# A hybrid decoder layer on one core: left-side tiles moved up by 128 bytes, and attention's small tiles in a pool of their own

## The chip, the cores and the metric

The kernel runs on one core of one Trainium2 chip. Its time is the device time of one execution, in microseconds (us); lower is better. TensorE (PE) multiplies, and its weight loads are listed apart as PEld; VectorE is DVE, ScalarE is ACT, GpSimd is POOL, and SyncE (SP) issues the DMAs.

## The reference

One layer over 1024 tokens of width 1024, all in float32. `A` are eight heads with a sliding window of 128, ALiBi and sinks, `B` are eight heads of causal attention with a forget gate; both read one projection of RMSNorm(x).

```python
xn = rmsnorm(x, attn_norm_g)
proj = jnp.einsum('bsd,de->bse', xn, w_in)
qa, ka, va, qb, kb, vb, f_logit = jnp.split(proj, IN_SPLITS, axis=-1)
...
out_a = swa_sinks_attention(qa, ka, va, sink_logits)
...
out_b = forgetting_attention(qb, kb, vb, log_f)
mixed = jnp.concatenate([out_a.reshape(b, s, A_Q_W), out_b.reshape(b, s, B_W)], axis=-1)
x = x + jnp.einsum('bse,ed->bsd', mixed, w_out)
hn = rmsnorm(x, mlp_norm_g)
hid = jnp.square(jax.nn.relu(jnp.einsum('bsd,df->bsf', hn, w_up)))
x = x + jnp.einsum('bsf,fd->bsd', hid, w_down)
```

## The kernel before

**Arithmetic.** Each float32 product is three passes in float32r: both operands are split into a high and a low part (`split`, lines 73 to 78), and hi·hi, hi·lo and lo·hi are added up in PSUM. All products go through the helper `mm` (line 71), so they stand under L71 and are told apart by their tiles. In `mm(out, lhsT, rhs)` the second argument is the stationary operand, loaded as weights before each matmul, and the third is the moving operand, streamed past it; most moving tiles are 512 columns wide.

**Stages.** The first projection (`qps`, lines 162 to 192) and the later ones (`ps`, function `proj`) take tokens `xh`, `xl` as weights and the split weights `wh`, `wl` as moving tiles of 384 or 392 columns. Attention's scores (`sp`, `spb`) take queries (`q1a`, `q1b`) as weights, and keys (`k1a`, `k1b`, and their low part `k2z`) move. The probabilities are turned by transposes (`tpa`, `tpb`), in which the probabilities are the weights and `ident` moves. The turned ones (`pth`, `ptl`) move past the values `va`, `vb` (`pv`, `pvb`). The output projection (`po`) takes `wos` as weights past `mix`. Both halves of the MLP are done by Strassen-Winograd products, seven for eight. Up (`up`, line 969 onwards) runs 16 steps `j`; each makes seven pairs of weights `wu`, four blocks of 128 columns, and moves `bh` and `bl` past them: 84 matmuls of 512 columns into `pu`, in the order wu hi·bh, wu hi·bl, wu lo·bh. Down (`down`) runs 16 steps over four phases; per product it splits `hx` and `wx` and makes 24 matmuls of 512 columns into `pd`, in the same order of three. Both have 1344 matmuls.

**Where tiles lie.** In a partition of SBUF, pools with `side="left"` stack upwards and pools with `side="right"` stack down from byte 229,344; a tile's bytes are rounded up to 32. The left side begins at byte 2,176 with pool `cp`, whose tiles come in the order of their declarations: `ident`, `ident_b`, `ones1`, `vt` (36 floats, 160 bytes with rounding), then nothing larger than 256 bytes, 2,528 bytes in all. So the pools behind it (`xg_p` and `wp`, later `zl` in their place) begin at byte 4,704, which is 96 modulo 256. All slots of `zl` are multiples of 2,048 bytes long: everything in it, `wu`, `wos`, `mix` and the left-side slots of `hx` and `wx` among it, begins at 96 modulo 256. On the right side `ap1` (q, k, v after projection; `va`, `vb`) holds multiples of 256 bytes and lies at 224 modulo 256. `ap2` under it mixes large tiles with small ones of 4 to 64 bytes: in between these, `q1a`, `q1b` and the bias tiles come to lie at 64 modulo 256, and `k1a`, `k1b`, `k2z`, `pth`, `ptl` and the probabilities at 192. Pool `zr`, which takes the place of `ap1` and `ap2` after attention, holds multiples of 256 bytes again: `bh`, `bl` and the right-side slots of `hx` and `wx` lie at 224. `ident` lies at 128.

In `down` a set of `hx` and `wx` is always from one pool: the first four sets alternate left, right, left, right (`FIRST`), and after them all are on the left (`SETS`).

**What sets the order.** The program's order is laid by a planner that plays the kernel on a timeline of its own and takes what is ready by priority; `tc.high_priority` and `tc.issue_after` push and hold, and `PACE` spreads the projections over attention. A tile waits for a free slot of its tag, and tiles of `zl` and `zr` wait for those earlier tiles that lay at the same bytes (`reuse_waits="tile"`).

Of the kernel before, what the change touches and what calls it, by code (L numbers as in the profile page):

```python
# [8 lines left out]
F32 = mybir.dt.float32  # L9
# [7 lines left out]
P = 128  # L17
# [3 lines left out]
NT = S // P  # L21
HD = 64
NH = 8
# [30 lines left out]
def hybrid_layer(  # L54
# [13 lines left out]
    nc = tc.nc  # L68

    def mm(out, lhsT, rhs, start, stop):  # L70
        return nc.tensor.matmul(out, lhsT, rhs, start=start, stop=stop)  # L71
# [20 lines left out]
    cp = ctx.enter_context(tc.tile_pool(name="cp", bufs=1))  # L92
# [8 lines left out]
    ones1 = cp.tile([P, 1], F32, name="ones1")  # L101
    nc.vector.memset(ones1, 1.0)

    vt = cp.tile([P, 36], F32, name="vt")
    nc.scalar.dma_start(vt, vecs)
    nc.scalar.preload_act_table_set("natural_log_exp_and_others")
    ga, gm, vec, bfb, snk = (
        vt[:, a:b] for a, b in ((0, 8), (8, 16), (16, 20), (20, 28), (28, 36))
# [31 lines left out]
    at = ExitStack()  # L140
    ap1 = at.enter_context(tc.tile_pool(name="ap1", bufs=1, side="right"))
    ap2 = at.enter_context(tc.tile_pool(name="ap2", bufs=1, side="right"))
    maskd = ap2.tile([P, P], F32, tag="mt", name="maskd", bufs=2)
    nc.gpsimd.memset(maskd, 0.0)
    nc.gpsimd.affine_select(
# [82 lines left out]
    def qknorm(x, nh, tlo, thi, r=None):  # L228


        n = thi - tlo
        w = nh * HD
        sq = ap2.tile([P, 1024], F32, tag="sq", name="sq", bufs=1)
        sqv = sq[:, : n * w].rearrange("p (t c) -> p t c", t=n)
        xv = x[:, tlo:thi, :w]
        nc.gpsimd.tensor_tensor(out=sqv, in0=xv, in1=xv, op=ALU.mult)
        ss, r0, u = (
            ap2.tile([P, 16], F32, tag=tag, name=tag, bufs=2)[:, : n * nh]
            for tag in ("ss", "sr0", "su")
        )  # L240
        nc.vector.tensor_reduce(
            out=ss, in_=sq[:, : n * w].rearrange("p (g d) -> p g d", d=HD),
            axis=AX.X, op=ALU.add,
        )
        th = lambda a: a.rearrange("p (t h) -> p t h", h=nh)
        nc.vector.scalar_tensor_tensor(
            out=th(ss), in0=th(ss), scalar=1.0 / HD,
            in1=ep2[:, tlo:thi].unsqueeze(2).to_broadcast([P, n, nh]),
            op0=ALU.mult, op1=ALU.add,
        )  # L250
        nc.scalar.activation(r0, ss, AF.Ln)
        nc.scalar.activation(r0, r0, AF.Exp, scale=-0.5)
        nc.vector.tensor_tensor(out=u, in0=r0, in1=r0, op=ALU.mult)
        nc.vector.tensor_tensor(out=u, in0=u, in1=ss, op=ALU.mult)
        na = nh + (2 if r is not None else 0)
        if r is None:
            rv = ap2.tile([P, 16], F32, tag="r", name="r", bufs=2)[:, : n * nh]
            rv = th(rv)
        else:
            rv = r[:, tlo:thi, :]  # L260
        nc.vector.scalar_tensor_tensor(
            out=rv[:, :, :nh], in0=th(u), scalar=3.0, in1=th(r0),
            op0=ALU.subtract, op1=ALU.mult,
        )
        for t in range(n):
            xt = x[:, tlo + t, : na * HD].rearrange("p (h d) -> p h d", d=HD)
            nc.gpsimd.tensor_tensor(
                out=xt, in0=xt, in1=rv[:, t].unsqueeze(2).to_broadcast([P, na, HD]), op=ALU.mult
            )
# [110 lines left out]
    for t in range(0, NT, 4):  # L380
        qknorm(q0, 4, t, t + 4, rqk)
# [41 lines left out]
    def forget_gates():  # L423
        zf = z.rearrange("p h t -> p (h t)")

        zt = ap2.tile([P, 4, NT * NH], F32, tag="sq", name="zt", bufs=1)
        ze, zs, zp = zt[:, 0], zt[:, 1], zt[:, 2]
        nc.vector.scalar_tensor_tensor(out=ze, in0=zf, scalar=-1.0, in1=zf, op0=ALU.mult, op1=ALU.min)
        nc.scalar.activation(ze, ze, AF.Exp)
        nc.vector.tensor_scalar(out=zs, in0=ze, scalar1=2.0, scalar2=None, op0=ALU.add)  # L430
        nc.vector.reciprocal(zs, zs)
        nc.vector.tensor_tensor(out=zs, in0=zs, in1=ze, op=ALU.mult)
        nc.vector.tensor_tensor(out=ze, in0=zs, in1=zs, op=ALU.mult)
        nc.vector.tensor_scalar_mul(zp, ze, 2.0 / 17.0)
        for n in (15, 13, 11, 9, 7, 5, 3):
            nc.vector.scalar_tensor_tensor(
                out=zp, in0=zp, scalar=2.0 / n, in1=ze, op0=ALU.add, op1=ALU.mult
            )
        nc.vector.scalar_tensor_tensor(out=zp, in0=zp, scalar=2.0, in1=zs, op0=ALU.add, op1=ALU.mult)
        nc.vector.scalar_tensor_tensor(  # L440
            out=zt[:, 3], in0=zf, scalar=0.0, in1=zp,
            op0=ALU.min, op1=ALU.subtract,
        )
        pt = pa.tile([P, 512], F32, tag="tr", name="ptf", bufs=2)
        nc.tensor.transpose(pt[: NH * NT, :P], zt[:, 3], ident)
        cum = ap2.tile([NH * NT, P], F32, tag="rdt", name="cum", bufs=1)
        nc.vector.tensor_tensor_scan(
            out=cum, data0=ones1[: NH * NT].to_broadcast([NH * NT, P]),
            data1=pt[: NH * NT, :P], initial=0.0, op0=ALU.mult, op1=ALU.add,
        )  # L450
        off = pa.tile([P, 512], F32, tag="tr", name="off", bufs=2)
        mm(
            off[: NH * NT, 0:1], before.rearrange("p h t -> p (h t)"),
            cum[:, P - 1 : P], True, True,
        )
        offs = ap2.tile([NH * NT, 1], F32, name="offs")
        nc.vector.tensor_copy(offs, off[: NH * NT, 0:1])
        nc.vector.tensor_scalar(
            out=cum, in0=cum, scalar1=offs[:, 0:1], scalar2=None, op0=ALU.add
        )  # L460
        nc.sync.dma_start(c_d.rearrange("h (t q) -> (h t) q", q=P), cum)
# [163 lines left out]
    def scores_b(p, qp, h):  # L625
        q1, k1, k2, cb = heads[p, "q"][h], heads[p, "k1", h], k2_of[h], heads[p, "cb", h]
        probs = []
        for i in (2 * qp, 2 * qp + 1):
            nk = (i + 1) * P
            pr = ap2.tile(  # L630
                [P, S if i > 3 else 512], F32, tag="s" if i > 3 else "u", name="sb",
                bufs=NS if i > 3 else NU,
            )
            nm = ap2.tile([P, 4], F32, tag="nm", name="nmb", bufs=4)
            dn = ap2.tile([P, 4], F32, tag="dn", name="dnb", bufs=4)
            qs = q1[:, i * P : (i + 1) * P]
            for c in range((nk + 511) // 512):
                n = min(512, nk - c * 512)
                ne = max(n, 256)
                ks = slice(c * 512, c * 512 + ne)  # L640
                sp = pa.tile([P, 512], F32, tag="sc", name="spb", bufs=2)
                last = (c + 1) * 512 >= nk
                mm(sp[:, :ne], qs, k1[:, ks], True, False)
                mm(sp[:, :ne], qs, k2[:, ks], False, not last)
                if last:
                    pe = mm(sp[:, n - P : n], ident_b, mask_b, False, True)
                nc.vector.tensor_tensor_reduce(  # L647
                    out=pr[:, c * 512 : c * 512 + n], in0=sp[:, :n],
                    in1=cb[:, c * 512 : c * 512 + n], scale=1.0,
                    scalar=3e38 if c == 0 else nm[:, 0:1],  # L650
                    op0=ALU.add, op1=ALU.min, accum_out=nm[:, c : c + 1],
                )
            nc.scalar.activation(
                pr[:, :nk], pr[:, :nk], AF.Exp, scale=-1.0, bias=nm[:, c : c + 1],
                accum_out=dn_b[p % 2][:, h, i : i + 1] if p < 3 else dn[:, 0:1],
            )
            probs.append(pr)
            if p < 3:
                continue
            nc.vector.reciprocal(dn[:, 1:2], dn[:, 0:1])  # L660
            if i > 1:
                nc.vector.tensor_scalar_mul(pr[:, :nk], pr[:, :nk], dn[:, 1:2])
            else:
                nc.gpsimd.tensor_tensor(
                    out=pr[:, :nk], in0=pr[:, :nk],
                    in1=dn[:, 1:2].to_broadcast([P, nk]), op=ALU.mult,
                )
        marks.append(pe.ins)
        return probs
# [221 lines left out]
    left, right = slice(0, 512), slice(512, 1024)  # L891
# [328 lines left out]
    for i in range(len(STEPS)):  # L1220
        down(i)
        if STEPS[i][0] == len(PHASES) - 1 and late:
            name, dt, cs = late.pop(0)
# [63 lines left out]
```

## Time and profile before

| | us |
|---|---|
| three runs: lowest, median, highest | 1122.52, 1126.16, 1127.7 |
| the profiled execution | 1124.34 |
| its span, first to last instruction | 1122.6 |
| up in the chain that ended last (`pu`, two pieces) | 181.77 and 117.12 |
| down in the same chain (`pd`) | 300.64 |

The profile is of one execution. Its busy time counts an engine as busy while an instruction's record lasts; matmul records overlap, since each begins before the record of the one ahead has ended. So the pace of a stretch of matmuls is read from the stretch's length and its count, and not from the mean record. The chain that ended last is followed back from the last instruction, each time to what released it. A matmul's row by tile gives the shortest, the median and the longest record.

### The profile page before, as it was taken

To read this page: it belongs to the slowest core of one execution; us is meant where nothing else is said; L and a number is where in the kernel's file an instruction comes from. 1 tells how busy PE (TensorE), PEld (TensorE's weight loads), DVE (VectorE), ACT (ScalarE), POOL (GpSimd) and SP (SyncE) were. 2 spreads that over 40 slices of the span, in tenths; PEclk is the share of its full clock that TensorE was granted. 3 is DMA by queue.
4 is the path that set the end of the run, shared out by engine and by line. 5 is a ranking of instruction groups with operands and counts; after the bars stand their busy time and mean duration, and the time that the engine had idled before them with its cause. 6 is when DMAs were issued, how large, how long until landed. Compare 5 with 4: busy or idle time off the path is not lost.

```text
span 1122.6 us, 15570 instructions
## 1 busy us (share of the span) xinstructions
PE 1098.7 (98%) x5551; PEld 937.5 (84%) x5551; DVE 765.4 (68%) x1311; ACT 575.4 (51%) x1013; POOL 361.0 (32%) x338
## 2 busy tenths in 40 slices
PE   9999998999999999899999999999999999999998
PEld 8999988799997888777888887888888888888886
DVE  7476665765667577699867677855575876674395
ACT  5567557766677656455454534344444433333331
POOL 4751613335434545124232323222221222222100
PEclk9999999999999999999999999999999999999999
DMA  9311302314438656473454544335699786665523
GB/s 312 124 36 37 95 24 59 96 29 142 153 120 312 203 182 219 168 236 131 173 194 169 196 151 159 134 121 194 227 392 351 258 299 244 216 230 205 173 95 113
DMA packets 95710, 195.68 MB, mean 174 GB/s; under 512 B 7136, under 2 KB 19088, under 8 KB 95632
## 3 DMA queue, kind: packets, MB, share of 16 engines
q1 hardware_dynamic: 95488, 194.66, 49.6%
q8 instruction: 44, 0.72, 0.3%
q14 instruction: 34, 0.28, 0.1%
q10 hardware_dynamic: 144, 0.02, 0.0%
HBM read 141.61 MB, written 53.04 MB: 173 GB/s over the span
## 4 chain that ended last, share of the span: by engine, by line
PE 83%; DVE 7%; issue 4%; DMA 4%; POOL 1%; ACT 1%; SPq 0%; DVEq 0%; ACTq 0%; POOLq 0%
PE pd L71 27%; PE pu L71 27%; PE ps L71 12%; PE po L71 4%; PE qps L71 3%; PE spb L71 3%; PE pvb L71 2%; PE tpb L683 2%; PE sp L71 1%; DVE ptl L360 1%; DMA mixs_d<-mixs 1%; DVE sb L647 1%; DVE bl L78 1%; PE pv L71 1%; DMA wr<-in_w_b_dram 1%
## 5 line engine op out<-in xcount | busy, mean ns | idle before, releaser
L71 PE MATMUL pd<-hx,wx 128*128 128x512 f32 x1344 | 304.9, 389 | 0.0
L71 PEld LDWEIGHTS pd<-hx,wx 128*128 128x128 f32 x1344 | 252.3, 188 | 52.4
L71 PE MATMUL pu<-bh,wu 128*128 128x512 f32 x896 | 281.6, 395 | 0.8 <-ACT wu L75 0.8
L71 PEld LDWEIGHTS pu<-bh,wu 128*128 128x128 f32 x896 | 168.8, 188 | 40.7 <-ACT wu L75 1.2
L71 PE MATMUL pu<-bl,wu 128*128 128x512 f32 x448 | 176.9, 395 | 0.5 <-DVE bl L78 0.5
L75 ACT CAST hx<-hr 128x1024 fp32r<-128x1024 f32 x56 | 59.0, 1054 | 176.2 <-PE pd L71 171.3
L78 POOL TENSOR_TENSOR wx<-wda,wx 128x1024 fp32r<-128x1024 f32 x24 | 64.5, 2687 | 197.0 <-ACT wx L75 197.0
L78 DVE TENSOR_TENSOR hx<-hr,hx 128x1024 fp32r<-128x1024 f32 x56 | 72.7, 1305 | 73.5 <-ACT hx L75 73.4
L71 PE MATMUL ps<-wh,xh 128*128 128x384 f32 (+1 forms) x320 | 110.2, 345 | 0.3 <-ACT qkb L600 0.3
L71 PE MATMUL ps<-wh,xl 128*128 128x384 f32 (+1 forms) x320 | 109.3, 342 | 0.0
L71 PE MATMUL ps<-wl,xh 128*128 128x384 f32 (+1 forms) x320 | 109.1, 342 | 0.0
L71 PEld LDWEIGHTS pu<-bl,wu 128*128 128x128 f32 x448 | 84.4, 188 | 21.1 <-DVE bl L78 0.9
L71 PE MATMUL po<-mix,wos 128*128 128x512 f32 x384 | 95.8, 400 | 3.7 <-DMA mix<-mixs_d 1.6
L78 POOL TENSOR_TENSOR wu<-wus,wu 128x512 fp32r<-128x512 f32 x32 | 48.0, 1501 | 133.4 <-ACT wu L75 133.4
L71 PEld LDWEIGHTS po<-mix,wos 128*128 128x128 f32 x384 | 70.9, 190 | 18.3 <-DMA mix<-mixs_d 1.8
L75 ACT CAST wu<-wus 128x512 fp32r<-128x512 f32 x64 | 39.0, 618 | 79.4 <-PE pu L71 76.0
L78 POOL TENSOR_TENSOR wu<-wur,wu 128x512 fp32r<-128x512 f32 x32 | 43.3, 1354 | 88.2 <-ACT wu L75 88.2
L360 DVE TENSOR_TENSOR ptl<-tpb,pth 128x512 fp32r<-128x512 f32 (+1 forms) x80 | 50.0, 632 | 25.9 <-ACT pth L359 25.2
L965 DVE TENSOR_TENSOR ht<-hb 128x512 f32<-128x512 f32 x32 | 21.8, 722 | 64.7 <-ACT hb L1020 64.7
L78 POOL TENSOR_TENSOR wl<-wr,wh 128x384 fp32r<-128x384 f32 (+1 forms) x47 | 49.9, 1076 | 48.8 <-ACT wh L75 36.9
L75 ACT CAST wx<-wda 128x1024 fp32r<-128x1024 f32 x56 | 58.3, 1044 | 7.2 <-DMA wda<-in_w_d_dram 6.6
L71 PEld LDWEIGHTS ps<-wh,xh 128*128 128x128 f32 x320 | 60.4, 189 | 1.1 <-ACT qkb L600 0.6
(218 smaller groups left out, 2058.4 us busy)
## 6 DMA issues: line engine op xcount, KB each, us to landing
wda<-in_w_d_dram SPq DMA_DIRECT2D x34, 1024.0 KB, 9.0
hr<-hid_d SPq DMA_DIRECT2D x56, 512.0 KB, 5.8
wur<-in_w_u_dram SPq DMA_DIRECT2D x32, 512.0 KB, 4.4
hid_d<-ht SPq DMA_DIRECT2D x16, 1024.0 KB, 4.3
hid_d<-hb SPq DMA_DIRECT2D x16, 768.0 KB, 3.6
mixs_d<-mixs SPq DMA_DIRECT2D x14, 512.0 KB, 3.4
mix<-mixs_d SPq DMA_DIRECT2D x7, 1024.0 KB, 8.7
wr<-in_w_b_dram SPq DMA_DIRECT2D x32, 192.0 KB, 2.4
```

Of the source, the lines that this page charges most:

```text
L71: return nc.tensor.matmul(out, lhsT, rhs, start=start, stop=stop)
L75: hi_eng.copy(hi, src)
L78: lo_eng.tensor_tensor(out=lo, in0=src, in1=hi.bitcast(F32), op=ALU.subtract)
L360: nc.vector.tensor_tensor(out=lo[:, cols], in0=pt[:, cols], in1=hi[:, cols].bitcast(F32), op=ALU.subtract)
L647: nc.vector.tensor_tensor_reduce(out=pr[:, c * 512 : c * 512 + n], in0=sp[:, :n], in1=cb[:, c * 512 : c * 512 + n], scale=1.0, scalar=3e38 ...
L683: nc.tensor.transpose(tp[:, c0 : c0 + P], probs[qi][:, kb * P : (kb + 1) * P], ident)
L965: eng.tensor_tensor(out=out, in0=a, in1=b, op=ALU.subtract)
```

## The change

`vt` is made 68 floats wide instead of 36, of which the load and all readers still use the first 36. With rounding it grows from 160 to 288 bytes, so that all that stands behind it on the left side lies 128 bytes further: the pools behind `cp` begin at 4,832, or 224 modulo 256. `ident`, `ident_b`, `ones1` and `vt` itself stay where they are. The small tiles of `ap2` (`ss`, `sr0`, `su`, `r`, `offs`, `nm`, `dn`; 800 bytes) go to a new pool `ap3`, opened after `ap2` and so under it. All that stays in `ap2` then lies at 224 modulo 256. `ap1` and `zr` stay where they are. No instruction is added, removed or moved in the text of the program.

```diff
-    vt = cp.tile([P, 36], F32, name="vt")
-    nc.scalar.dma_start(vt, vecs)
+
+
+    vt = cp.tile([P, 68], F32, name="vt")
+    nc.scalar.dma_start(vt[:, :36], vecs)
...
     ap2 = at.enter_context(tc.tile_pool(name="ap2", bufs=1, side="right"))
+
+    ap3 = at.enter_context(tc.tile_pool(name="ap3", bufs=1, side="right"))
...
-            ap2.tile([P, 16], F32, tag=tag, name=tag, bufs=2)[:, : n * nh]
+            ap3.tile([P, 16], F32, tag=tag, name=tag, bufs=2)[:, : n * nh]
             for tag in ("ss", "sr0", "su")
...
-            rv = ap2.tile([P, 16], F32, tag="r", name="r", bufs=2)[:, : n * nh]
+            rv = ap3.tile([P, 16], F32, tag="r", name="r", bufs=2)[:, : n * nh]
...
-        offs = ap2.tile([NH * NT, 1], F32, name="offs")
+        offs = ap3.tile([NH * NT, 1], F32, name="offs")
...
-            nm = ap2.tile([P, 4], F32, tag="nm", name="nmb", bufs=4)
-            dn = ap2.tile([P, 4], F32, tag="dn", name="dnb", bufs=4)
+            nm = ap3.tile([P, 4], F32, tag="nm", name="nmb", bufs=4)
+            dn = ap3.tile([P, 4], F32, tag="dn", name="dnb", bufs=4)
```

Distances between the moving operand and the weights, modulo 256:

| matmuls | columns | before | after |
|---|---|---|---|
| `pu` (up) | 512 | 128 | 0 |
| `pd` (down), `po` | 512 | 0 | 0 |
| `pd`, the last matmul of each of the first four sets, against the next set's weights | 512 | 128 | 0 |
| `pv`, `pvb` | 512, 256 | 32 | 0 |
| `sp`, `spb` | 256 to 512 | 128 | 0 |
| `qps`, `ps` | 384, 392 | eight values, in steps of 32 | the same eight |
| transposes of probabilities | 128 | 64 | 96 |

## The prediction

> **What bounds the kernel now.** I read the page first: who is busy, and of what the chain that ended last is made.
>
> ```profile
> PE 1098.7 (98%) x5551; PEld 937.5 (84%) x5551; DVE 765.4 (68%) x1311; ACT 575.4 (51%) x1013; POOL 361.0 (32%) x338
> ...
> PE 83%; DVE 7%; issue 4%; DMA 4%; POOL 1%; ACT 1%; SPq 0%; DVEq 0%; ACTq 0%; POOLq 0%
> PE pd L71 27%; PE pu L71 27%; PE ps L71 12%; PE po L71 4%; PE qps L71 3%; PE spb L71 3%; PE pvb L71 2%; PE tpb L683 2%; PE sp L71 1%; DVE ptl L360 1%; DMA mixs_d<-mixs 1%; DVE sb L647 1%; DVE bl L78 1%; PE pv L71 1%; DMA wr<-in_w_b_dram 1%
> ```
>
> PE carries 83% of the chain, and up and down carry 27% each. So the next view is the chain in order of time, from the start of up (start, length, what, how many).
>
> ```profile
> 512.40 181.77 PE pu L71 x781
> 694.17 1.72 PE pms L71 x4
> 695.88 117.12 PE pu L71 x504
> 813.01 300.64 PE pd L71 x1326
> 1113.67 0.71 DVE pd L1204
> ```
>
> From 512 us to 1114 us PE waits for nobody: what a matmul there costs is what the kernel costs. The two stages do the same kind of matmul, 512 columns in three float32r passes, and do not run at the same pace. Up: 181.77 + 117.12 = 298.89 us for 1285 matmuls, 232.6 ns each. Down: 300.64 us for 1326, 226.7 ns each. So the question is why a matmul of up takes 5.9 ns more, and whether the change takes that away.
>
> **Is it other engines' traffic?** Next come windows of 20 us: busy time and count by engine, granted clock, DMA share, GB/s. The first two lie in up, the others in down.
>
> ```profile
> 740.00:760.00 20.00, 20.00 (x88) 16.22 (x87) 12.24 (x18) 8.93 (x11) 5.64 (x5) 1.00 0.42 156
> 780.00:800.00 20.00, 20.00 (x88) 16.21 (x87) 10.10 (x17) 7.74 (x10) 3.88 (x3) 1.00 0.36 133
> 820.00:840.00 20.00, 20.00 (x90) 16.56 (x89) 14.63 (x12) 5.74 (x6) 5.87 (x2) 1.00 1.05 393
> 1080.00:1100.00 20.00, 20.00 (x90) 16.57 (x89) 20.00 (x18) 7.67 (x8) 0.00 (x0) 1.00 0.56 194
> ```
>
> The clock is 1.00 in all four. Down holds its 90 matmuls with the DMAs full (1.05) and POOL at work, and with DVE busy for the whole window; up gets 88 with DVE at half and DMA at 0.36. Other engines' load does not explain it. What differs is where the operands lie: in down both are at one offset modulo 256, in up they are 128 apart.
>
> **Does the offset itself show?** The records by tile (shortest, median, longest, ns) stand below for up, down, and attention's product with the values. The two-matmul row is down again, in a window of 0.2 us around the end of its first set: the next set's weights are on the other side.
>
> ```profile
> L71 PE MATMUL pu<-bh,wu x896: 390/393/797, 496.7 to 812.6; 128*128 128x512 f32 x180
> ...
> L71 PE MATMUL pd<-hx,wx x1344: 388/389/398, 812.8 to 1117.3; 128*128 128x512 f32 x192
> ...
> L71 PE MATMUL pv<-pth,va x30: 388/398/506, 86.5 to 211.2; 128*128 128x512 f32 x30
> ...
> L71 PE MATMUL pd<-hx,wx x2: 389/392/396, 817.9 to 818.1; 128*128 128x512 f32 x2
> ```
>
> Down, at distance 0, has a median of 389; up, at 128, has 393. In the two-matmul row one record of 389 stands beside one of 396: the same tiles and stage, and the only matmul there during which weights 128 apart are loaded costs 7 more. That crossing also changes sides, so I look for a case on one side: `pv` has both operands on the right, 32 apart, and its median is 398. Unequal offsets cost, then, also without a change of side, though attention's rows hold stalls too.
>
> **Part 1, the left side 128 bytes further.** The distance in up goes from 128 to 0. If its matmuls then run at down's pace, 1285 × 226.7 ns = 291.3 us take the place of 298.89: 7.6 us less, all of it on the chain. The 59 other matmuls of up's 1344 lie before 512.40, where the chain runs through DVE: I count nothing for them. The four crossings in down are worth 4 × 7 ns, nothing.
>
> What is late next, if PE runs 2.5% faster? The window over up's longer piece, and the longest wait for PE in up:
>
> ```profile
> 513.00:694.00 181.00, 181.00 (x780) 146.76 (x779) 131.41 (x195) 85.97 (x110) 54.92 (x38) 1.00 0.46 167
> ...
> ACT wu L75 <- PE pu L71: 102.0, 52, 2.2
> ```
>
> The busiest other engine in up is DVE, 131.41 of 181 us; it would rise from 73% to about 75%. The weight splits on ACT wait for PE to give slots back (102.0 us in 52 waits), so the feed has slack. The tightest spot is the start of down, which moves 7.6 us ahead:
>
> ```profile
> 808.32 1.05 ACT L75 CAST wx<-wda 128x1024 fp32r<-128x1024 f32 x1 [5.37 <-DMA wda<-in_w_d_dram]
> ...
> L78 POOL TENSOR_TENSOR wx<-wda,wx x3: 2412/2605/3368, 801.0 to 821.7; 128x1024 fp32r<-128x1024 f32 x3
> ```
>
> The second set's weights are cast at 808.32, after 5.37 us of waiting for their DMA, and POOL adds at most 3.4 us: ready at about 813, used at 818.1. That is 5 us of cover. The slots that these loads wait for come free in the last step of up, so they move ahead with it; only the part of up's gain that falls after the release is lost to the loads, 84 × 5.9 ns = 0.5 us for a whole step. The cover holds. If it were gone, PE would stand still once for what is missing, not for every set.
>
> **Part 2, attention's tiles at one offset.** 156 matmuls of 512 columns go from 32 or 128 apart to 0: 60 in `pv`, 48 each in `spb` with `k1b` and `k2z`.
>
> ```profile
> L71 PE MATMUL spb<-k2z,q1b 128*128 128x512 f32 x48 | 19.0, 396 | 0.0
> ...
> L683 PE MATMUL tpb<-ident,sb 128*128 128x128 f32 x288 | 44.6, 273 | 0.1
> L288 PE MATMUL ptq<-ident,q 128*128 128x128 f32 x32 | 5.5, 273 | 0.0
> ...
> L71 PE MATMUL sp<-k1a,q1a x64: 274/281/389, 58.1 to 176.4; 128*128 128x256 f32 x64
> ...
> L71 PE MATMUL pvb<-pth,vb x160: 277/281/415, 212.6 to 459.8; 128*128 128x256 f32 x160
> ```
>
> At 396 and 398 against 389 they cost 7 to 9 ns too much: 156 × 8 = 1.2 us, of which I take 0.5, because attention's chain changes often between PE, DVE and POOL. The 256-wide ones (`sp`, `pvb`, some of `spb`, about 500) have no row at equal offsets; from median to shortest is 281 − 274 = 7 ns, so ±3.6 us of PE time and about a third of that on the chain; I take 0 and keep ±1.2 for the range. The transposes go from 64 to 96 apart; `ptq` turns tiles of `ap1`, which are 96 apart already, at the same 273 ns: no price.
>
> **What has one answer.** `qps`, `ps`, `po` and down's own pairs keep their distances. VectorE, ScalarE and GpSimd work from tiles at new addresses; ScalarE's casts of `wh` go through eight offsets already, and all lie close together:
>
> ```profile
> L75 ACT CAST wh<-wr x40: 498/512/525, 25.7 to 273.4; 128x384 fp32r<-128x384 f32 x32, 128x392 fp32r<-128x392 f32 x8
> ...
> L896 ACT ACTIVATE bh<-h,vt x10: 707/722/725, 462.1 to 497.4; 128x512 fp32r<-128x512 f32 x10
> ...
> 429.93 0.97 POOL sb L664 x2
> ```
>
> The new pool changes one order: `ap3` lies under slot c0 of `zr`, so `bh1` now waits for the last reader of `nm` and `dn`. That is the scaling of the last probabilities, on DVE and POOL; POOL's piece stands in the chain at 429.93, and `bh` is first written at 462.1. It costs nothing.
>
> **Sum.** 7.6 + 0.5 = 8.1 us off: the profiled execution (1124.34, that is 1.7 around its span) goes to 1116.2. The median of the three runs, 1126.16, is 1.8 above the profiled one; on that footing the forecast is 1118. About 0.5%, 5.6 us, is what a measurement of this kernel can tell from no change.
>
> **The rivals.** *The offset is not the cause* (0.16). In down, operands at distance 0 modulo 256 are at 0 modulo 512 too, since their slots are multiples of 2,048 apart and their steps are 512; in up the change leaves them 256 apart modulo 512 (4,832 + 40,960 against 100,320), and on two sides. If 512 counts, or the side, up stays at 232.6 ns and the time at 1124.3, or 1126 as a median, less at most attention's 1.2. For it: only the crossing and attention separate the offset from the stage, and neither separates it cleanly. Against it: `pv` on one side. The Trainium skill speaks for this rival: its page "TensorE: Matmul & The Clock Gate", section "Step-by-step: what each phase is for", gives PE two independent read ports and says that loading the next weights "doesn't steal SBUF read bandwidth from the running matmul". By that rule no address could matter and the change would be worth 0. The trace's 389 beside 396 within one stage does not agree with it.
>
> *The new distance is a worse one* (0.07), the slower side. If operands at 256 modulo 512 on two sides collide as those of `pv` do, up's median goes from 393 to 398: 1285 × 5 ns = 6.4 us more, 1130.7, or 1132.6 as a median. It decides from 5.6 us / 1285 = 4.4 ns a matmul on.
>
> **How the numbers follow.** The forecast has 0.77. Its own spread, attention's bounds and the runs' scatter, reaches from 1114 to 1122; nearly all of it is faster by over 0.5%, so faster is 0.75, the rest of it and the first rival make 0.18 for no change, and the second rival 0.07 for slower. The range 1114 to 1124 holds the forecast and the low edge of the first rival.
>
> **What would show it.** Right: up's two pieces of the chain together at about 291 us for 1285 matmuls, `pu`'s medians at 389, 90 matmuls to 20 us in up, no 396 at the crossing, down unchanged at 226.7 ns and without a wait at its start. Wrong: `pu` still at 393 (the first rival) or above (the second), or a gain in up that comes back as a wait for `wda` or `hr` at the start of down. Medians of `pv` and `spb` at 389 would carry part 2.

## The result and the profile after

| | before | changed |
|---|---|---|
| median of six runs, us | 1127.09 | 1116.87 |
| lowest to highest, us | 1122.52 to 1129.03 | 1116.02 to 1118.19 |
| the profiled execution, us | 1124.34 | 1117.92 |

The ratio is 0.9914 (95% interval 0.9894 to 0.9934): about 9.7 us faster. Of the five executions of a kernel further down, the one with slot m2 longer, one took 2801.81 us and the other four 1120.31 to 1122.77; the ratio there leaves it out, and nothing on record tells its cause. The instructions of every engine are the same, in the same order, as before; only addresses differ, and the waits that follow from them.

The chain that ended last, in order of time, from the start of up (start, length, what, how many):

```profile
513.34 177.32 PE pu L71 x781
690.66 1.72 PE pms L71 x4
692.38 114.29 PE pu L71 x504
806.67 300.57 PE pd L71 x1326
1107.27 0.71 DVE pd L1208
```

Up's two pieces are 291.61 us for the same 1285 matmuls, 226.9 ns each, where they were 298.89 us and 232.6 ns. Down is what it was, 300.57 against 300.64. Up begins 0.9 us later than in the profile of before, so the profiled span is 6.4 us shorter, though up alone gives 7.3. The same windows of 20 us as before (busy time and count by engine, granted clock, DMA share, GB/s):

```profile
740.00:760.00 20.00, 20.00 (x90) 16.57 (x89) 13.23 (x20) 8.47 (x10) 6.55 (x5) 1.00 0.39 145
780.00:800.00 20.00, 20.00 (x90) 16.57 (x89) 9.91 (x14) 8.43 (x9) 5.12 (x3) 1.00 0.47 164
820.00:840.00 20.00, 20.00 (x90) 16.57 (x89) 12.50 (x10) 5.85 (x7) 2.49 (x1) 1.00 1.05 391
1080.00:1100.00 20.00, 20.00 (x90) 16.57 (x89) 17.18 (x16) 6.73 (x7) 0.00 (x0) 1.00 0.43 158
```

Up now has 90 matmuls to the window, as down has. The records by tile (shortest, median, longest, ns), and the scores' second pass by form (busy us, mean ns):

```profile
L71 PE MATMUL pu<-bh,wu x896: 388/389/793, 498.4 to 806.3; 128*128 128x512 f32 x180
...
L71 PE MATMUL pd<-hx,wx x1344: 388/389/389, 806.5 to 1110.9; 128*128 128x512 f32 x192
...
L71 PE MATMUL pv<-pth,va x30: 387/397/503, 87.0 to 214.5; 128*128 128x512 f32 x30
...
L71 PE MATMUL spb<-k2z,q1b 128*128 128x512 f32 x48 | 19.0, 395 | 0.0
```

Up's median is down's 389. Down's longest record is 389 too: the crossings of 396 are gone. Attention's rows have not followed (397 and 395, before 398 and 396). The start of down is covered as it was: the second set's weights are cast at 802.45 after a wait of 5.22 us for their DMA, and PE's idle time before down's matmuls is 0.0 us in the profile.

```profile
802.45 1.06 ACT L75 CAST wx<-wda 128x1024 fp32r<-128x1024 f32 x1 [5.22 <-DMA wda<-in_w_d_dram]
```

### The profile page after: what moved, and what is told of

It is laid out like the page before. It is cut to its first block, busy times and chain, and to the rows that moved or that the text cites. A ratio compares the mean times of both kernels' runs of the same rounds, so it can differ in the third digit from the quotient of the medians.

```text
span 1116.2 us, 15570 instructions
## 1 busy us (share of the span) xinstructions
PE 1090.6 (98%) x5551; PEld 936.8 (84%) x5551; DVE 769.2 (69%) x1311; ACT 573.2 (51%) x1013; POOL 361.4 (32%) x338
## 4 chain that ended last, share of the span: by engine, by line
PE 82%; DVE 8%; DMA 4%; issue 2%; ACT 2%; POOL 1%; SPq 0%; DVEq 0%; ACTq 0%; POOLq 0%
PE pd L71 27%; PE pu L71 26%; PE ps L71 12%; PE po L71 5%; PE spb L71 3%; PE pvb L71 2%; PE tpb L687 2%; PE sp L71 2%; DMA xq<-in_x_dram 1%; PE pv L71 1%; PE tpa L523 1%; DVE ptl L364 1%; DVE bl L78 1%; DMA wr<-in_w_b_dram 1%; DVE bl L901 1%
## 5 line engine op out<-in xcount | busy, mean ns | idle before, releaser
L71 PE MATMUL pu<-bh,wu 128*128 128x512 f32 x896 | 276.6, 390 | 0.2 <-ACT wu L75 0.2
L71 PE MATMUL pu<-bl,wu 128*128 128x512 f32 x448 | 174.3, 390 | 0.8 <-DVE bl L78 0.8
```

## The experiments

The theory: what a 512-wide matmul costs in this stream depends on the distance, modulo 256, between the bytes at which the moving operand and the weights begin. The rivals: crossing from one side to the other costs; the distance counts modulo 512; the place of one operand alone counts, and not the distance; attention's tiles carry part of the gain. Unless said otherwise each is an edit of the kernel before, and "distance" is that between up's operands.

**The left side alone.**

```diff
-    vt = cp.tile([P, 36], F32, name="vt")
-    nc.scalar.dma_start(vt, vecs)
+    vt = cp.tile([P, 68], F32, name="vt")
+    nc.scalar.dma_start(vt[:, :36], vecs)
```

> The left side 128 bytes further, attention's small tiles left where they were. Theory (the distance between up's moving tiles and weights, modulo 256, sets its pace): up at 226.7 to 227 ns a matmul instead of 232.6, the whole gain of the change, ratio 0.991 to 0.993. Rival (attention's tiles carry part of it): less than that, by about 0.5 us of it.

Measured: ratio 0.992 (0.9908 to 0.9933), median 1116.26 us. Its chain:

```profile
511.10 177.34 PE pu L71 x781
688.44 1.72 PE pms L71 x4
690.16 114.29 PE pu L71 x504
```

Up's pieces are within 0.02 us of the changed kernel's. The left side's move is enough for the whole gain that can be measured.

**The pool alone.** The changed kernel with `vt` back at 36 floats.

> Attention's small tiles in their own pool, the left side where it was. Theory: up stays at 232.6 ns, the 512-wide matmuls of attention stay where they were, ratio 1.000 within 0.003. Rival (equal distance pays in attention too): 0.5 to 1.2 us less, ratio 0.999, and the median of the product with the values falls from 398 to 389 ns.

Measured: ratio 0.9989 (0.9978 to 1.0).

```profile
499.79 191.06 PE pu L71 x821
690.85 1.72 PE pms L71 x4
692.57 117.13 PE pu L71 x504
809.70 300.66 PE pd L71 x1326
```

Up is at 308.19 us for 1325 matmuls, 232.6 ns, as before (the chain is followed further back into up here, so it holds 40 more of them). The interval ends at 1.0, so a gain of a microsecond can neither be shown nor excluded by the time; attention's rows speak against one:

```profile
L71 PE MATMUL pv<-pth,va x30: 390/397/505, 86.8 to 211.2; 128*128 128x512 f32 x30
...
L71 PE MATMUL spb<-k2z,q1b 128*128 128x512 f32 x48 | 18.9, 395 | 0.0
```

**Distance or side?** Slot m2 is made 128 bytes longer, so that the left slots behind it move: `wu` comes to distance 0 from `bh`, and in down the left set with moving `r0` and weights `m0` comes to distance 128 on one side.

```diff
-        m = mixt[e] = slot(MIX[e], f"mix{e}", [2, S], F32R)
+        pad = 32 if MIX[e] == "m2" else 0
+        m = slot(MIX[e], f"mix{e}", [2 * S + pad], F32R)
+        m = mixt[e] = m[:, : 2 * S].rearrange("p (c s) -> p c s", c=2)
```

> Slot m2 of the left pool 128 bytes longer, nothing else moved: up's weights come to distance 0, and in down the first of three left-side sets (moving r0, weights m0) comes to distance 128 with both operands on the left. Theory (distance modulo 256, whatever the side): up at 227 ns; in down 431 of 1344 matmuls cost 6 ns more, so down takes 303.2 us in the chain instead of 300.6, with medians unchanged but many records of 393 to 396. Rival (crossing from one side to the other is what costs): up stays at 232.6 ns and down at 300.6 us.

Measured: ratio 0.9966 (0.9953 to 0.9979).

```profile
513.59 177.36 PE pu L71 x781
690.95 1.72 PE pms L71 x4
692.67 114.30 PE pu L71 x504
806.97 304.13 PE pd L71 x1326
```

Up crosses sides still and runs at 227.0 ns. Down loses 3.5 us with both operands on the left (304.13 against 300.64). The side rival falls. The two effects add up: 7.2 us off up and 3.5 us on down leave 3.7 us, and the ratio is worth 3.8 us of 1126. Down's loss was forecast at 2.6 us; spread over the forecast's 431 matmuls it is 8 ns each instead of 6, and why that is more than up pays at the same distance stays open. The output projection shows the same from the other end: in this kernel most of its pairs come to distance 128, and its median goes from the 389 of before to 393.

```profile
L71 PE MATMUL po<-mix,wos x384: 387/393/628, 351.6 to 498.2; 128*128 128x512 f32 x192
```

**Is it the move, or where it ends?** The left side 256 and 384 bytes further: `vt` with 100 and with 132 floats, loaded as above. The first brings the distance back to 128, the second makes it 0 modulo 512.

> The left side 256 bytes further instead of 128. Theory (modulo 256): distance is 128 again, up at 232.6 ns. Rivals: if any move of the left side helps, or if the distance counts modulo 512 only, up leaves 232.6 ns.

> The left side 384 bytes further than before: up's operands at distance 0 modulo 512 too, where the changed kernel leaves 256. If 256 modulo 512 costs nothing: up at the changed kernel's 226.9 ns a matmul. If it costs something: below that.

With 256:

```profile
513.68 182.49 PE pu L71 x781
696.17 1.72 PE pms L71 x4
697.88 117.12 PE pu L71 x504
```

With 384:

```profile
510.61 179.58 PE pu L71 x790
690.19 1.72 PE pms L71 x4
691.90 114.29 PE pu L71 x504
```

At 256 the gain is gone (233.2 ns; one execution, 1126.33 us). At 384 the second piece is 114.29 us, the changed kernel's to the hundredth (one execution, 1117.45 us). So it is the distance modulo 256 that counts; whether it is 0 or 256 modulo 512 makes no difference.

**The price by distance.** The left side 32, 64, 96 and 192 bytes further: `vt` with 44, 52, 60 and 84 floats.

> The left side 32 bytes further: up's moving tiles lie 96 bytes from its weights, modulo 256. Theory A (only distance 0 is free, any other costs the same): up at 232.6 ns a matmul. Theory B (the price grows with the distance up to 128): between 230 and 232.6 ns.

> The left side 64 bytes further: distance 64. Theory A: 232.6 ns. Theory B: about half the price, 229 to 230 ns. Theory C (what counts is the distance modulo 64): 226.7 ns.

> The left side 96 bytes further: distance 32. Theory A: 232.6 ns. Theory B: a quarter of the price, about 228 ns. Theory C: as at 96.

> The left side 192 bytes further: the weights lie 64 bytes behind the moving tiles instead of ahead, modulo 256. If only the size of the distance counts, the same pace as at 64; theory A: 232.6 ns; if the order of the two streams counts, another pace than at 64.

Each ran once: 1126.87, 1119.67, 1126.67 and 1126.30 us. The second piece of up (504 matmuls) in each, in that order, and above the first of them the longer piece of the same run:

```profile
513.57 182.50 PE pu L71 x781
...
697.78 117.60 PE pu L71 x504
```
```profile
692.86 115.37 PE pu L71 x504
```
```profile
697.65 117.60 PE pu L71 x504
```
```profile
697.33 117.59 PE pu L71 x504
```

| moving operand's first byte less the weights', modulo 256 | 0 | 32 | 64 | 96 | 128 | 192 |
|---|---|---|---|---|---|---|
| ns a matmul, the second piece's length / 504 | 226.8 | 233.3 | 228.9 | 233.3 | 232.4 | 233.3 |

Theory A comes nearest: at 32, 96, 128 and 192 the price is 5.6 to 6.5 ns. The 5.6 at 128 is not a lower price of that distance: in the run 256 bytes further, at 128 too, the longer piece takes 182.49 us, as it does at 96 (182.50), where the kernel before took 181.77. But 64 costs only 2.1, and 64 the other way (192) the full price, so the order of the two counts. That the price grows with the distance (B) and that the distance counts modulo 64 (C) both fall. Why 64 is cheap stays open.

In up the moving operand stays at 224 in all of these, and only the weights move; so up alone can't tell the distance from the weights' own place. Down can: on the left, where all but two of its sets lie, both operands move, to 128, 160, 192 and 32, and their distance stays 0. Its piece in the same four runs:

```profile
815.38 300.81 PE pd L71 x1326
```
```profile
808.23 300.73 PE pd L71 x1326
```
```profile
815.24 300.73 PE pd L71 x1326
```
```profile
814.92 300.70 PE pd L71 x1326
```

That is 226.8 to 226.9 ns a matmul, with 226.7 before. Weights at 128, 192 or 32 are slow past a moving operand at 224 and not past one at their own remainder: the distance counts, and not the place.

**Attention: is it the transposes?** On top of the changed kernel, the identity 96 bytes further, so that the transposes between attention's products are at distance 0 as well; `vt` is shortened, so that all behind it stays (`ident_b`, `ones1` and `vt` itself, which lie between, move by 96 bytes too).

```diff
-    ident = cp.tile([P, P], F32, name="ident")
+    ident = cp.tile([P, 24 + P], F32, name="ident")[:, 24:]
...
-    vt = cp.tile([P, 68], F32, name="vt")
+    vt = cp.tile([P, 44], F32, name="vt")
```

> The changed kernel with the identity moved 96 bytes further, so that attention's transposes have both operands at distance 0 as well. Theory (the transposes between them, still 96 apart, are what keeps attention's 512-wide matmuls slow): the median of the product with the values falls from 397 to 389 ns, the mean of the scores' second pass from 395 to 389, and the time by 1 us, ratio to the kernel before 0.990. Rival (their excess is short runs and waits, not the offset): rows and time as in the changed kernel, ratio 0.991 to 0.992.

Measured: ratio 0.9929 (0.9904 to 0.9954).

```profile
L687 PE MATMUL tpb<-ident,sb 128*128 128x128 f32 x288 | 45.6, 278 | 0.0
...
L71 PE MATMUL spb<-k2z,q1b 128*128 128x512 f32 x48 | 19.2, 400 | 0.0
```

The means of 400 and 278, where the changed kernel has 395 and 272, are no price of an address. For 3.4 us in attention this execution ran at half the clock (the 0.50 in the window below), and a few long records lie there: one of the 48 of the scores takes 628 ns, which by itself lifts their mean by 5, and ten of the 288 transposes, six here and four in a second such stretch at 454.5 us, take 392 to 418.

```profile
341.90:345.30 3.40, 3.40 (x17) 3.00 (x16) 3.14 (x11) 1.96 (x4) 1.48 (x5) 0.50 1.02 417
...
L71 PE MATMUL spb<-k2z,q1b x1: 628/628/628, 344.4 to 344.4; 128*128 128x512 f32 x1
...
L687 PE MATMUL tpb<-ident,sb x6: 392/417/418, 341.9 to 343.6; 128*128 128x128 f32 x6
```

The medians are untouched: 397 for `pv`, 272 for the transposes, as in the changed kernel. The offset of the transposes is not what holds attention's matmuls above 389.

**The projections at one distance.** On top of the changed kernel, all slots of `wh` at distance 0 from the tokens; room is made with two slots for `wr`. The control has two slots and nothing else.

```diff
-        return [
-            wp.tile([P, WN], dt, tag=tag, name=tag, bufs=n)
-            for tag, dt, n in (("wr", F32, 3), ("wh", F32R, 8), ("wl", F32R, 8))
-        ]
+        wh, wl, wr = [
+            wp.tile([P, n], dt, tag=tag, name=tag, bufs=bufs)
+            for tag, dt, bufs, n in (
+                ("wh", F32R, 8, 448), ("wl", F32R, 8, WN), ("wr", F32, 2, WN)
+            )
+        ]
+        return [wr, wh, wl]
```

> The changed kernel with the eight slots of wh 1792 bytes long, so that all of wh lies at distance 0 from the tokens; room for it is made by two slots for wr instead of three. Theory (unequal distances cost the projections too): 768 of 1152 matmuls of 384 columns go from 174 to 177 ns down to 173.5, 1 to 2 us less than the changed kernel, ratio 0.990. Rival (at 384 columns the offset is hidden, or the lost slot costs more): no gain, ratio 0.991 or above.

> The changed kernel with two slots for wr instead of three and nothing else: the control for the run with wh aligned. If the third slot is not needed: as the changed kernel, ratio 0.991 to 0.992. If it is: the projections' loads come later and the time rises by 1 us or more.

Measured: 0.998 (0.9967 to 0.9993) aligned, 0.9985 (0.9972 to 0.9998) in the control. Aligned:

```profile
518.93 177.34 PE pu L71 x781
```
```profile
L71 PE MATMUL ps<-wh,xh 128*128 128x384 f32 x256 | 87.9, 346 | 0.8 <-ACT wh L75 0.5 <-ACT qkb L607 0.3
...
L71 PE MATMUL ps<-wl,xh 128*128 128x392 f32 x64 | 22.7, 354 | 3.7 <-POOL wl L78 3.7
```

Control:

```profile
518.56 177.32 PE pu L71 x781
```
```profile
L71 PE MATMUL ps<-wh,xh 128*128 128x384 f32 x256 | 87.8, 345 | 0.9 <-ACT wh L75 0.6 <-ACT qkb L604 0.3
...
L71 PE MATMUL ps<-wl,xh 128*128 128x392 f32 x64 | 23.0, 359 | 3.9 <-POOL wl L78 3.9
```

The two ratios differ by less than either interval, and the 384-wide matmuls have means of 346 and 345: no gain from the distance can be seen at 384 columns. What both lose against the changed kernel comes with the third slot: up begins 5 us later (518.9 and 518.6 against 513.3), PE waits 3.7 to 3.9 us for the split `wl` on POOL, and the planner lays a different order. Both profiles also have a lower granted clock than the changed kernel's (0.995 against 0.998); how much of the 5 us is the wait and how much the clock, no run separates. No version tried beats the changed kernel by more than its interval.

## Why the prediction was right, point by point

*Where the kernel is bound.* Right: from up's start to down's end PE waits for nobody, before and after, and the 7.3 us that up lost came out in the profiled span, less the 0.9 by which up began later.

*Up at down's pace.* Right: forecast 291.3 us at 226.7 ns, measured 291.61 at 226.9. The gain there is 7.3 us against 7.6. The two medians at 389, the 90 matmuls to 20 us and the missing crossing of 396 are as forecast.

*The argument from load.* Right: down keeps its 90 matmuls to the window under full DMA, and with slot m2 longer a set of down loses its pace when nothing but addresses change.

*The argument from one side.* Its conclusion, that the offset costs without a crossing, is shown by down with slot m2 longer. The row that I took for it was wrong: `pv`'s median of 398 had next to nothing to do with its distance of 32, since it is 397 at distance 0. (The moving tiles lay 32 behind the weights there, 224 modulo 256, a distance that no run of up has.) Its excess may come from the short runs or the waits in attention; no run here tells.

*Attention's 512-wide matmuls, 0.5 us.* Wrong: the term was built on those rows and is not to be seen (395 against 396, 397 against 398).

*What has one answer.* Right: down's pace, the cover at its start, and the order of all engines are unchanged.

*The first rival*, that the address does not matter or counts modulo 512, falls with the result and with the run 384 bytes further. What spoke for it was the rule of the Trainium skill's page "TensorE: Matmul & The Clock Gate", section "Step-by-step: what each phase is for", that a weight load takes no read bandwidth from the running matmul. The runs do not agree with what the prediction drew from it, that no address could matter: with the same instructions a matmul takes 226.8 ns at distance 0, 228.9 at 64, and 232.4 to 233.3 at four other distances. What the two reads share inside the chip, the runs don't show. *The second rival*, a worse distance, falls too: its price was taken from `pv`.

*The sum.* Forecast 1118 as a median, measured 1116.87; forecast 8.1 us off, measured about 9.7. Of the sum's two terms up's is right (7.6 forecast, 7.3 measured), and attention's 0.5 is not to be seen. The rest of the gain was in no term, so that the median came within 1.1 us is in part luck. The ratio of the left side alone, 0.992 (0.9908 to 0.9933), is 7.5 to 10.4 us of 1126, a little more than up's 7.3 as well.

Some of this rest goes with the clock. It is 1.00 in up and down in every profile, but ahead of up ten of the fourteen profiled executions have one or more short stretches at half the clock. Windows on the one of the kernel before, the one of the changed kernel, and the same place with the left side alone, which has none:

```profile
452.20:455.60 3.40, 3.40 (x11) 2.77 (x11) 0.00 (x0) 0.00 (x0) 0.00 (x0) 0.50 0.02 6
```
```profile
131.50:134.90 3.40, 3.40 (x16) 3.40 (x15) 2.69 (x4) 2.74 (x11) 3.40 (x3) 0.50 0.60 212
```
```profile
131.50:134.90 3.40, 3.40 (x24) 3.19 (x22) 2.42 (x4) 2.37 (x9) 3.28 (x4) 1.00 0.74 221
```

The kernel before and the changed kernel have one each, and their profiled spans are 6.4 us apart. Of the executions on record with a granted clock of 1.000, the two of the kernel before took 1122.38 and 1122.51 us, and the three with the left side alone 1115.70, 1115.71 and 1116.26: 6.1 to 6.8 us apart, which leaves nothing above up's 7.3. At 0.996 the kernel before took 1126.09 to 1128.79. These are few executions, on different chips. The start of up follows the clock only in part: it is at 511.1 with the left side alone and at 513.3 in the changed kernel, but at 513.7 with the left side 256 bytes further, which has no such stretch ahead of up either. Why the clock falls in one execution and not in another, and whether the change has a part in it, no run separates.

## What to carry to other kernels

Where PE runs without gaps and loads new weights under each matmul, compare the pace of its stages as length over count, not as mean records: two stages of equal shape at 226.7 and 232.6 ns ask for a cause, and the bytes at which the operands begin are one. Give moving operand and weights the same remainder modulo 256, for instance by padding one small tile in front of a pool; it costs a few bytes and no instruction. The gain is shown here for matmuls of 512 columns in float32r. Before taking a slow row as evidence for a cause, look whether it also holds waits, or a few records from a stretch of low clock, which move a mean and not a median.

## What the runs showed that was not expected

The price of a distance is not a matter of its size: 32 bytes cost as much as 96 or 192 (233.3 ns), and 64 costs 2.1 ns where 192, 64 the other way, costs 6.5. At 384 columns no gain from distance 0 showed, while at 512 it is 2.5%. And with one slot fewer for `wr` up began 5 us later and the median rose from 1116.87 to 1123.82 us, more than half of what the whole change brings, though part of that goes with a lower clock.
